# Sparse attention beside the recurrence: two of its steps instead of three per weight unit

## The chip, the cores and the metric

The kernel runs on one core of one Trainium2 chip. The metric is the device time of one execution in microseconds (us). The median of three runs before the change is 1681.42 us (1681.36 to 1682.54).

## The reference, cut to what matters

The program is one block of a first model and two layers of a second one, for 256 tokens of width 1024. The change touches the mixer of the first block alone. That mixer computes two groups of outputs from the same normalised input, joins them and projects them:

```
parts = jnp.split(h @ w_in, IN_SPLITS, axis=-1)
nq, k_c, v_c, k_s, v_s, k_w, v_w, gl, hq, hf, hi, hg = parts
o_nsa = nsa_group(nq, k_c, v_c, k_s, v_s, k_w, v_w, gl, ...)   # sparse attention, 8 heads of 64
o_hg  = hgrn2_group(hq, hf, hi, hg, lower_bound, hg_norm)      # gated recurrence, 4 heads of 128
return jnp.concatenate([o_nsa, o_hg], axis=-1) @ w_out
```

The sparse attention adds three branches, each weighted by a gate: attention to the selected blocks, to the window, and to 15 compressed blocks. With 256 tokens the first two see every earlier token. The recurrence multiplies its state path with `hi` and gates its normalised output with `hg`.

## The kernel before, in words

The 256 tokens are two tiles of 128, called T=0 and T=1. Each tile is a Python generator (`net(T)`) that writes the whole program for that tile; `run` lets T=0 go ahead and T=1 follow some steps behind, so that one weight unit in SBUF serves both. A generator yields the name of the weight unit that it wants next, or None for a step without weights.

A weight unit is one or two pieces of up to 256 KB, which come on SyncE's queue into 6 buffers `wr`. Each piece is split by ScalarE (L319, the rounded high part) and VectorE (L320, the rest) into a pair out of 42 buffers `w`, and a product of activations and weights is three matmuls (`mm3`, L348 to L350, here called weight matmuls, type fp32r). A pair of `w` is free again when T=1 has used it, and ScalarE's split of a later piece waits for that.

Inside the mixer, `merge(main, side, per)` writes `main` up to its next weight unit, then `per` steps of `side`:

```
def merge(main, side, per=1):
    ...
        while True:
            u = yield tag
            tag = main.send(u)
            for _ in range(per):
                next(side, None)
    ...
    for _ in side:
        yield None
```

`main` is `hgrn_out` here: the product `hi` (4 weight units), the recurrence's output (L903, L905), its mean square (ScalarE L907, L912, VectorE L453, GpSimd L455, VectorE L925), the product `hg` (4 units), the gate (ScalarE L922, VectorE L923, L924, L926) and the transpose of the result (`to_xT`: L358, then L353 and L354). `side` is `nsa_attn`: four blocks, one for each of two branches and two halves of the heads, then the compressed branch, then the transpose. A block is three steps: scores (L986) and softmax (VectorE L656, then ScalarE L658, for four heads); transposes of the first probabilities (L358) and a copy (`pT`, ScalarE L673 or VectorE L671), then the first products with the values (L1002); the rest of them and the weighted sum (L962, L963, L970, L974). The compressed branch is L1012, L1019 to L1032, a transpose, L1036 and the sum. In all `nsa_attn` has 14 yields.

After the mixer's two groups comes `out_proj("wo")`, whose weights are 8 row blocks: the first four belong to the attention's half of the input, the last four to the recurrence's half.

PSUM has, for each tile, one bank `mm`, one `tr` and two `a`. Matmuls that are not weight matmuls (type f32: L358, L986, L1002, L903, L905, L1012, L1036) are called f32 matmuls below. The order of the instructions on each engine is fixed when the program is built: a planner orders what the generators write, and functions marked `urgent`, `to_xT` among them, are put ahead.

Of the kernel before, what the change touches and what calls it, by code (L numbers as in the profile page):

```python
# [241 lines left out]
def merge(main, side, per=1):  # L242
    ret = None
    try:
        tag = next(main)
# [5 lines that stand above are left out]
    except StopIteration as e:  # L251
        ret = e.value
    for _ in side:
        yield None
    return ret
# [9 lines left out]
class Net:  # L265
# [416 lines left out]
    def mixer1(self, T, xT, done):  # L682
        nc, sh, c = self.nc, self.sh, self.c
        kn = P * (T + 1)
        tk = slice(P * T, P * T + P)
        oT = self.xt_tiles()


        pz = yield from self.dense("hf", xT, 4, 512)
        zc = self.s2()  # L690
        nc.vector.tensor_scalar(zc, pz, -69.0776, None, op0=OP.max)
        l = self.s2()
        nc.scalar.activation(l, zc, AF.Abs)
        nc.scalar.activation(l, l, AF.Exp, scale=-1.0)
        nc.scalar.activation(l, l, AF.Ln, bias=1.0)
        logf = self.s2()
        nc.vector.scalar_tensor_tensor(logf, zc, 0.0, l, op0=OP.min, op1=OP.subtract)
        nlk = zc
        nc.vector.scalar_tensor_tensor(nlk, zc, 0.0, l, op0=OP.max, op1=OP.add)
        bp = self.pt("tr")  # L700
        for h in range(4):
            nc.tensor.matmul(bp[:, P * h:P * h + P], logf[:, P * h:P * h + P], c["tri"],
                             start=True, stop=True)
        bT = self.s2()
        nc.scalar.activation(bT, bp, AF.Copy)
        up = self.pt("tr")
        for h in range(4):
            self.tr(up[:, P * h:P * h + P], nlk[:, P * h:P * h + P])
        uT = self.s2()
        nc.vector.scalar_tensor_tensor(uT, up, -1.0, bT, op0=OP.mult, op1=OP.subtract)  # L710
        if T == 0:
            kx = self.keep(P, 4).rearrange("p h t -> p (h t)")
            for h in range(4):
                nc.scalar.activation(kx[:, P * h:P * h + P], uT[:, P * h:P * h + P], AF.Exp,
                                     bias=bT[:, P * h + P - 1:P * h + P])
            sh["kx"] = kx


        pz = yield from self.dense("hq", xT, 4, 512, bank="a")
        qs = self.s2()  # L720
        nc.scalar.activation(qs, pz, AF.Tanh, scale=0.5)
        nc.vector.scalar_tensor_tensor(qs, qs, 1.0, pz, op0=OP.add, op1=OP.mult)
        tp = self.pt("tr")
        for h in range(4):
            self.tr(tp[:, P * h:P * h + P], qs[:, P * h:P * h + P])
        qT = self.s2()
        nc.scalar.activation(qT, tp, AF.Copy, scale=0.5)


        pz = yield from self.dense("kk", xT, 4, 512)  # L730
        kk = self.s2()
        nc.scalar.activation(kk, pz, AF.Copy)
        if T == 0:
            sh["kc2"] = self.keep(P, 4)
            sh["nkT"] = self.keep(S, 2)
            sh["nv"] = self.keep(S, 2)
            sh["kcb"] = self.t("kcb", [P, 2, 16], 1)
            nc.gpsimd.memset(sh["kcb"], 0.0)
        cp = self.pt("tr")
        for g in range(4):  # L740
            for lp in range(2):
                nc.tensor.matmul(cp[64 * lp:64 * lp + 64, 64 * g:64 * g + 64],
                                 kk[:, 64 * g:64 * g + 64], c["sel"][:, 64 * lp:64 * lp + 64],
                                 start=True, stop=True)
        kc2 = sh["kc2"]
        nc.scalar.activation(kc2[:, :, 64 * T:64 * T + 64],
                             cp[:, 0:256].rearrange("p (g t) -> p g t", g=4), AF.Copy)
        tp = self.pt("tr")
        for i in range(2):
            self.tr(tp[:, P * i:P * i + P], kk[:, 256 + P * i:256 + P * i + P])  # L750
        nkT = sh["nkT"]
        nc.scalar.activation(nkT[:, :, tk], tp[:, 0:256].rearrange("p (b t) -> p b t", b=2), AF.Copy)

        yield from merge(self.nsa_proj(T, xT, nsa := {}),
                         self.hgrn_levels(T, bT, uT, qT, hg := {}))
        yield from merge(self.hgrn_out(T, xT, hg, oT), self.nsa_attn(T, nsa, oT), 3)
        yield from self.out_proj("wo", [oT], 8, W_WO, done)

    def compress(self):
# [806 lines left out]
```

## Time and profile before

| | |
|---|---|
| median of three runs | 1681.42 us |
| the profiled execution: its time, its span | 1679.82 us, 1678.0 us |
| TensorE busy | 1649.1 us, 98% |
| VectorE busy, ScalarE busy | 1111.4 us (66%), 937.1 us (56%) |
| DMA, mean share of 16 engines on the main queue | 55.8% |
| the chain that ended last | 87% TensorE, 6% VectorE, 3% DMA, 2% ScalarE |

A busy time sums the durations of an engine's instructions. Matmuls overlap, and their ends are modelled, so the distance from one matmul's start to the next one's start says more than a duration. The changed part of the program runs from about 283 to 381 us of the span.

### The profile page before, as it was taken

The numbers are of one execution on the slowest core, as the hardware profiler recorded it, in microseconds if no ns is written. First come the engines' busy times: TensorE is split into PE (matmuls) and PEld (weight loads), VectorE is DVE, ScalarE is ACT, GpSimd is POOL, SyncE is SP. The second block draws the span as 40 slices with busy tenths as digits, with TensorE's granted clock in tenths as the row PEclk, the third lists the DMA queues.
The fourth block names the chain that finished last, engine by engine and source line by source line (L and its number), as shares of the span: only waits on it lengthen the run. The fifth ranks groups of instructions, "written<-read, shape, count | busy, mean of one in ns | idle before, by whom it ended". The sixth has DMA issues, their size and how long they took to land.

```text
span 1678.0 us, 24853 instructions
## 1 busy us (share of the span) xinstructions
PE 1649.1 (98%) x8020; PEld 1343.1 (80%) x8020; DVE 1111.4 (66%) x2309; ACT 937.1 (56%) x1899; POOL 23.8 (1%) x43
## 2 busy tenths in 40 slices
PE   9999999999999999999999999999999999999997
PEld 7888777778888788887888888778888888788886
DVE  7666666676666766677557666885666865766666
ACT  7555655555555555555555555555555775555553
POOL 0000000000000000000000000000000000000000
PEclk9999999999999999999999999999999999999999
DMA  8856544336655566655436565565665633566652
GB/s 280 273 179 176 176 166 126 101 120 195 188 188 178 174 189 189 187 164 164 145 107 213 188 188 188 179 217 168 195 189 163 210 99 100 184 206 189 188 176 76
DMA packets 160547, 293.00 MB, mean 175 GB/s; under 512 B 18208, under 2 KB 27168, under 8 KB 160416
## 3 DMA queue, kind: packets, MB, share of 16 engines
q1 hardware_dynamic: 160128, 291.34, 55.8%
q8 instruction: 63, 1.03, 0.2%
q14 instruction: 68, 0.56, 0.1%
q10 hardware_dynamic: 288, 0.07, 0.0%
HBM read 290.29 MB, written 1.05 MB: 174 GB/s over the span
## 4 chain that ended last, share of the span: by engine, by line
PE 87%; DVE 6%; DMA 3%; ACT 2%; issue 2%; POOL 1%; DVEq 0%; POOLq 0%; SPq 0%; ACTq 0%
PE mm L348 16%; PE mm L350 15%; PE mm L349 15%; PE a L348 10%; PE a L349 9%; PE a L350 9%; PE tr L358 4%; DMA wr<-wp 2%; DVE w L320 1%; DVE x L555 1%; PE a L779 1%; ACT w L319 1%; DVE x L560 1%; DVE x L572 1%; PE a L1294 1%
## 5 line engine op out<-in xcount | busy, mean ns | idle before, releaser
L320 DVE TENSOR_TENSOR w<-wr,w 128x512 fp32r<-128x512 f32 (+3 forms) x1058 | 703.6, 679 | 351.9 <-ACT w L319 165.2
L319 ACT ACTIVATE w<-wr 128x512 fp32r<-128x512 f32 (+3 forms) x1058 | 649.3, 623 | 396.6 <-PE mm L349 233.3
L348 PE MATMUL mm<-w,xh 128*128 128x512 f32 (+3 forms) x1200 | 477.4, 398 | 0.6 <-DVE s L597 0.5
L350 PE MATMUL mm<-w,xl 128*128 128x512 f32 (+3 forms) x1200 | 464.8, 387 | 0.0
L349 PE MATMUL mm<-w,xh 128*128 128x512 f32 (+3 forms) x1200 | 463.8, 387 | 0.0
L348 PEld LDWEIGHTS mm<-w,xh 128*128 128x128 f32 x1200 | 225.7, 188 | 44.6 <-issue 4.4
L350 PEld LDWEIGHTS mm<-w,xl 128*128 128x128 f32 x1200 | 225.5, 188 | 43.3
L349 PEld LDWEIGHTS mm<-w,xh 128*128 128x128 f32 x1200 | 226.2, 189 | 38.7 <-issue 0.6
L348 PE MATMUL a<-w,s 128*128 128x512 f32 x531 | 208.1, 392 | 0.5 <-ACT s L353 0.5
L349 PE MATMUL a<-w,s 128*128 128x512 f32 x531 | 207.4, 391 | 0.0
L350 PE MATMUL a<-w,s 128*128 128x512 f32 x531 | 207.2, 391 | 0.2 <-DVE s L354 0.2
L348 PEld LDWEIGHTS a<-w,s 128*128 128x128 f32 x531 | 99.6, 188 | 25.0 <-issue 3.6
L348 PE MATMUL a<-w,xh 128*128 128x512 f32 (+2 forms) x304 | 118.8, 392 | 0.8 <-ACT xh L353 0.7
L349 PE MATMUL a<-w,xh 128*128 128x512 f32 (+2 forms) x304 | 118.0, 389 | 0.8 <-DVE w L320 0.7
L350 PE MATMUL a<-w,xl 128*128 128x512 f32 (+2 forms) x304 | 116.7, 387 | 0.0
L350 PEld LDWEIGHTS a<-w,s 128*128 128x128 f32 x531 | 99.6, 188 | 21.1 <-DVE s L354 0.6
L349 PEld LDWEIGHTS a<-w,s 128*128 128x128 f32 x531 | 99.7, 188 | 19.9
L353 ACT ACTIVATE s<-tr 128x256 fp32r<-128x256 f32 (+2 forms) x137 | 50.6, 371 | 70.8 <-PE tr L358 70.7
L354 DVE TENSOR_TENSOR s<-tr,s 128x256 fp32r<-128x256 f32 (+2 forms) x137 | 56.5, 413 | 47.9 <-ACT s L353 47.7
L358 PE MATMUL tr<-const,s 128*128 128x128 f32 (+1 forms) x436 | 77.5, 274 | 3.9 <-DVE s L595 1.8
L358 PEld LDWEIGHTS tr<-const,s 128*128 128x128 f32 (+1 forms) x436 | 55.9, 140 | 29.7 <-DVE s L472 2.7
L348 PEld LDWEIGHTS a<-w,xh 128*128 128x128 f32 x304 | 57.1, 188 | 14.8 <-ACT xh L353 3.3
(280 smaller groups left out, 1355.0 us busy)
## 6 DMA issues: line engine op xcount, KB each, us to landing
wr<-wp SPq DMA_DIRECT2D x994, 256.0 KB, 2.7
gb<-vec SPq DMA_DIRECT2D x21, 512.0 KB, 4.3
wr<-wp SPq DMA_DIRECT2D x32, 192.0 KB, 2.4
w<-wp SPq DMA_DIRECT2D x16, 256.0 KB, 5.3
wr<-wp SPq DMA_DIRECT2D x16, 160.0 KB, 2.4
wr<-wp SPq DMA_DIRECT2D x8, 168.0 KB, 2.3
wr<-wp SPq DMA_DIRECT2D x8, 140.0 KB, 2.1
out<-x SPq DMA_DIRECT2D x4, 256.0 KB, 2.0
```

The costliest lines, as they stand in the source:

```text
L319: nc.scalar.activation(hi[:, 0:w], r[:, 0:w], AF.Copy)
L320: nc.vector.tensor_tensor(lo[:, 0:w], r[:, 0:w], hi[:, 0:w].bitcast(FT), op=OP.subtract)
L348: mm(out, xh, wh, start=start, stop=False)
L349: mm(out, xh, wl, start=False, stop=False)
L350: mm(out, xl, wh, start=False, stop=stop)
L353: self.nc.scalar.activation(hi, src, AF.Copy)
L354: self.nc.vector.tensor_tensor(lo, src, hi.bitcast(FT), op=OP.subtract)
L358: self.nc.tensor.transpose(out, src, self.c["ident"][0:n, 0:n])
L555: nc.vector.scalar_tensor_tensor(y[:, cs], y[:, cs], nm, g[:, cs], op0=OP.add, op1=OP.mult)
L560: nc.vector.scalar_tensor_tensor(y[:, cs], y[:, cs], r, b[:, cs], op0=OP.mult, op1=OP.add)
L572: self.nc.vector.scalar_tensor_tensor(x[:, cs], acc, c, x[:, cs], op0=OP.mult, op1=OP.add, accum_out=s)
L779: nc.tensor.matmul(hp[0:2 * nb, 256 * kv:256 * kv + 256], kbs[kv][:, cc].rearrange("p g b -> p (g b)"), u[i][0], start=cc == 0, stop=cc == 15)
```

## The change

```
         yield from merge(self.nsa_proj(T, xT, nsa := {}),
                          self.hgrn_levels(T, bT, uT, qT, hg := {}))
-        yield from merge(self.hgrn_out(T, xT, hg, oT), self.nsa_attn(T, nsa, oT), 3)
+        yield from merge(self.hgrn_out(T, xT, hg, oT), self.nsa_attn(T, nsa, oT), 2)
         yield from self.out_proj("wo", [oT], 8, W_WO, done)
```

`hgrn_out` asks for 8 units, and `merge` writes attention steps after each of units 1 to 7. With three the attention is written out after five units; with two its 14 yields fill all seven places, and its last piece (the transpose of its result) is written after `hgrn_out` has ended, behind the transpose of the recurrence's result. The number of steps that `run` sees is the same, and so is the order of the weight units.

What moves on the engines. First TensorE, where T=1 does its third attention block and the recurrence's product. Before, `tr_974` and `tr_976` are the transposes of the block's probabilities (`se_...`), `a_973` its products with the values, `a_1008` the output projection of T=0 and `a_981` the recurrence's output of T=1:

```order
L348 MATMUL a_1008_3665<-w_3731,xh_2036 128x512
L349 MATMUL a_1008_3665<-w_3732,xh_2036 128x512
L350 MATMUL a_1008_3665<-w_3731,xl_2037 128x512
L358 MATMUL tr_974_3536<-const,se_3519 128x128 x2
L358 MATMUL tr_974_3536<-const,se_3523 128x128 x2
L358 MATMUL tr_976_3543<-const,se_3527 128x128 x2
L358 MATMUL tr_976_3543<-const,se_3531 128x128 x2
L1002 MATMUL a_973_3535<-keep_2425,pT_3541 128x64 x4
L1002 MATMUL a_973_3535<-keep_2425,pT_3548 128x64 x4
L903 MATMUL a_981_3572<-s_980_3570,s_700_2634 128x128
```

Now the same block's transposes are `tr_980` and `tr_982`; `mm_967` is the product `hg` of T=1, and `tr_985` the transpose of the recurrence's result of T=0:

```order
L358 MATMUL tr_980_3558<-const,se_3545 128x128 x2
L349 MATMUL mm_967_3533<-w_3287,xh_2233 128x512
L350 MATMUL mm_967_3533<-w_3286,xl_2234 128x512
L348 MATMUL mm_967_3533<-w_3290,xh_2233 128x512
L349 MATMUL mm_967_3533<-w_3291,xh_2233 128x512
L350 MATMUL mm_967_3533<-w_3290,xl_2234 128x512
L358 MATMUL tr_982_3565<-const,se_3549 128x128 x2
L358 MATMUL tr_982_3565<-const,se_3553 128x128 x2
L358 MATMUL tr_985_3588<-const,s_854_3182 128x128 x4
L1002 MATMUL a_979_3557<-keep_2425,pT_3563 128x64 x4
L1002 MATMUL a_979_3557<-keep_2425,pT_3570 128x64 x4
L358 MATMUL tr_986_3595<-const,s_799_3014 128x128 x4
```

Five weight matmuls now stand between the second and the third transposes, where none stood, and the transposes of T=0's two results (`tr_985`, `tr_986`) have come into this place.

Second TensorE, at the end of T=1's attention. Before, `tr_1020` is the transpose of the compressed branch, `a_1022` its product, `tr_1006` the transpose of the recurrence's result of T=0, and `a_1007` is T=0's output projection again:

```order
L350 MATMUL mm_986_3592<-w_3342,xl_2234 128x512
L358 MATMUL tr_1020_3701<-const,se_3689 128x128
L1036 MATMUL a_1022_3705<-s_774_2918,pT_3703 128x512
L358 MATMUL tr_1006_3657<-const,s_870_3223 128x128 x4
L348 MATMUL a_1007_3664<-w_3751,xh_2036 128x512
```

Now the compressed branch's transpose is `tr_1032`, its product `a_1034`, and T=0's output projection is `a_987` and `a_988`:

```order
L348 MATMUL a_987_3602<-w_3665,xh_2036 128x512
L349 MATMUL a_987_3602<-w_3666,xh_2036 128x512
L358 MATMUL tr_1032_3749<-const,se_3737 128x128
L350 MATMUL a_987_3602<-w_3665,xl_2037 128x512
L348 MATMUL a_988_3603<-w_3669,xh_2036 128x512
L1036 MATMUL a_1034_3753<-s_774_2918,pT_3751 128x512
L349 MATMUL a_988_3603<-w_3670,xh_2036 128x512
L350 MATMUL a_988_3603<-w_3669,xl_2037 128x512
```

Weight matmuls of T=0 now stand between the three f32 matmuls that stood in a row.

Third ScalarE, at the softmax of T=1's second block. Before:

```order
L353 ACTIVATE xh_2036<-tr_906_3327 128x512
L658 ACTIVATE se_3463,col_3456<-se_3463,col_3464 128x256
L658 ACTIVATE se_3467,col_3456<-se_3467,col_3468 128x256
L658 ACTIVATE se_3471,col_3456<-se_3471,col_3472 128x256
L658 ACTIVATE se_3475,col_3456<-se_3475,col_3476 128x256
L673 ACTIVATE pT_3485<-tr_957_3480 128x512
```

Now three splits and a copy of the product `hi` (L899) stand ahead of it:

```order
L319 ACTIVATE w_3768<-wr_3764 128x512
L319 ACTIVATE w_3772<-wr_3766 128x512
L319 ACTIVATE w_3814<-wr_3810 128x512
L899 ACTIVATE s_961_3511<-mm_899_3304 128x512
L658 ACTIVATE se_3456,col_3449<-se_3456,col_3457 128x256
L658 ACTIVATE se_3460,col_3449<-se_3460,col_3461 128x256
L658 ACTIVATE se_3464,col_3449<-se_3464,col_3465 128x256
L658 ACTIVATE se_3468,col_3449<-se_3468,col_3469 128x256
L673 ACTIVATE pT_3484<-tr_956_3479 128x512
```

On all engines together the numbers and shapes of the instructions are the same before and now, and their orders differ only from the first attention blocks up to the start of the next feed-forward part (`f2`).

## Rows read from the trace of the kernel before

**Rows 1.** The page: busy time of TensorE and its weight loads, VectorE, ScalarE, GpSimd (us, share of the span, instructions), and the granted TensorE clock in 40 slices of the span, in tenths of full speed.

```profile
PE 1649.1 (98%) x8020; PEld 1343.1 (80%) x8020; DVE 1111.4 (66%) x2309; ACT 937.1 (56%) x1899; POOL 23.8 (1%) x43
PEclk9999999999999999999999999999999999999999
```

**Rows 2.** Busy time by stretch, for 280 to 370 us: length of the stretch, TensorE, weight loads, VectorE, ScalarE, GpSimd, granted clock, DMA share, GB/s.

```profile
280.00:370.00 90.00, 85.28 (x488) 65.53 (x487) 58.11 (x172) 50.31 (x146) 2.32 (x4) 1.00 0.34 102
```

**Rows 3.** The instructions of TensorE in order of time (start, duration, line, tensors, shapes, count): the scores of T=0's first attention block, and the first matmul of the second chunk of `f2`. Between these two the order of TensorE changes; ahead of the one and from the other on it is the same.

```profile
283.28 0.72 PE L986 MATMUL a<-keep,s 64*128 64x128 f32 x8
...
381.45 0.39 PE L348 MATMUL mm<-w,xh 128*128 128x512 f32 x1
```

**Rows 4.** TensorE in order of time, three places: T=1's scores and the weight matmul behind them; products with the values and the two weight matmuls behind them; two weight matmuls in a row.

```profile
324.95 1.13 PE L986 MATMUL a<-keep,s 64*128 64x256 f32 x8
326.01 0.49 PE L348 MATMUL a<-w,xh 128*128 128x512 f32 x1
...
329.69 1.00 PE L1002 MATMUL a<-keep,pT 128*128 128x64 f32 x8
330.50 0.48 PE L349 MATMUL a<-w,xh 128*128 128x512 f32 x1
330.82 0.40 PE L350 MATMUL a<-w,xl 128*128 128x512 f32 x1
...
366.42 0.39 PE L350 MATMUL a<-w,xl 128*128 128x512 f32 x1
366.65 0.39 PE L348 MATMUL a<-w,xh 128*128 128x512 f32 x1
```

**Rows 5.** The place where T=0's fourth and T=1's first block begin, TensorE, VectorE and ScalarE in order of time; in brackets the engine's idle time before the instruction and what ended it.

```profile
306.95 0.69 DVE L925 TENSOR_TENSOR s<-s,col 128x512 f32<-128x512 f32 x1 [0.93 <-POOL col L455]
307.23 0.70 PE L986 MATMUL a<-keep,s 64*128 64x256 f32 x2
307.56 0.28 DVE L656 CUSTOM_DVE_ANT_0 se<-a,const 128x128 f32<-128x128 f32 x1
307.95 0.40 ACT L658 ACTIVATE se<-se,col 128x128 f32<-128x128 f32 x1 [1.34 <-DVE col L656]
308.49 0.33 PE L358 MATMUL tr<-const,se 128*128 128x128 f32 x1 [0.57 <-ACT se L658]
308.75 0.70 PE L986 MATMUL a<-keep,s 64*128 64x256 f32 x2
309.38 0.33 PE L358 MATMUL tr<-const,se 128*128 128x128 f32 x1
```

**Rows 6.** TensorE in T=1's first block.

```profile
319.67 0.48 PE L350 MATMUL mm<-w,xl 128*128 128x512 f32 x1
320.66 0.43 PE L1002 MATMUL a<-keep,pT 128*128 128x64 f32 x2 [0.51 <-ACT pT L673]
```

**Rows 7.** TensorE in T=1's third block.

```profile
334.38 0.40 PE L350 MATMUL a<-w,xl 128*128 128x512 f32 x1
335.02 0.93 PE L358 MATMUL tr<-const,se 128*128 128x128 f32 x4 [0.25 <-ACT se L658]
336.97 0.66 PE L358 MATMUL tr<-const,se 128*128 128x128 f32 x4 [1.03 <-ACT pT L673]
337.46 2.05 PE L1002 MATMUL a<-keep,pT 128*128 128x64 f32 x16
339.35 0.44 PE L903 MATMUL a<-s,s 128*128 128x128 f32 x2
```

**Rows 8.** TensorE at the end of T=1's attention.

```profile
352.86 0.40 PE L350 MATMUL mm<-w,xl 128*128 128x512 f32 x1
354.45 0.33 PE L358 MATMUL tr<-const,se 128*128 128x128 f32 x1 [1.20 <-ACT se L1027]
355.15 1.13 PE L1036 MATMUL a<-s,pT 128*128 128x512 f32 x2 [0.37 <-ACT pT L673]
356.11 0.60 PE L358 MATMUL tr<-const,s 128*128 128x128 f32 x4
357.40 0.50 PE L348 MATMUL a<-w,xh 128*128 128x512 f32 x1 [0.69 <-ACT xh L353]
```

**Rows 9.** ScalarE and VectorE behind the recurrence's product of T=1 (its last matmul's successor on TensorE starts at 341.29), with a copy `pT` ahead of it.

```profile
336.34 0.57 ACT L673 ACTIVATE pT<-tr 128x512 f32<-128x512 f32 x1
341.39 0.60 ACT L907 ACTIVATE s<-a 128x512 f32<-128x512 f32 x1 [3.99 <-PE a L905]
343.06 0.17 DVE L453 TENSOR_SCALAR col<-col 128x4 f32<-128x4 f32 x1 [2.62 <-ACT s L912]
344.35 0.69 DVE L925 TENSOR_TENSOR s<-s,col 128x512 f32<-128x512 f32 x1 [0.79 <-POOL col L455]
344.96 0.68 DVE L320 TENSOR_TENSOR w<-wr,w 128x512 fp32r<-128x512 f32 x1
345.56 0.42 DVE L656 CUSTOM_DVE_ANT_0 se<-a,const 128x256 f32<-128x256 f32 x1
346.02 0.51 ACT L658 ACTIVATE se<-se,col 128x256 f32<-128x256 f32 x1 [0.33 <-DVE col L656]
```

**Rows 10.** ScalarE at the softmax of T=0's second block: a split, and the first exponential behind it.

```profile
291.54 0.63 ACT L319 ACTIVATE w<-wr 128x512 fp32r<-128x512 f32 x1 [3.50 <-PE mm L349]
292.08 0.39 ACT L658 ACTIVATE se<-se,col 128x128 f32<-128x128 f32 x1
```

More of the change, by code (lines that the diff above doesn't have):

```diff
@@ L755, in mixer1 @@
                          self.hgrn_levels(T, bT, uT, qT, hg := {}))
-        yield from merge(self.hgrn_out(T, xT, hg, oT), self.nsa_attn(T, nsa, oT), 3)
+        yield from merge(self.hgrn_out(T, xT, hg, oT), self.nsa_attn(T, nsa, oT), 2)
         yield from self.out_proj("wo", [oT], 8, W_WO, done)
```

## The prediction

> **What bounds the kernel now.** The page comes first: TensorE is busy for 98% of the span, VectorE for 66%, ScalarE for 56%, and the granted clock is full in every slice [rows 1]. So the time is TensorE's, and a change of order can win only where TensorE stands still. The view by stretch then says how much that is where the change works: of the 90 us from 280 to 370, TensorE is busy for 85.28, at a granted clock of 1.00, which is the 2.4 GHz level [rows 2]. The number of instructions of each shape is the same before and after, so the sum is one of stalls, not of work. Between the first scores and the second chunk of `f2` lie 381.45 - 283.28 = 98.17 us [rows 3]; I ask how much of that is waiting, and how much will be.
>
> For that I read the third view, TensorE in order of time, from start to start. Prices without a wait: 0.23 for a weight matmul, 0.32 for one behind f32 matmuls, so that a change of kind costs some 0.1; 0.81 for four products with the values; 1.06 for T=1's scores, 0.27 for a quarter of them [rows 4]; 0.49 for four transposes, from the start of the second four to what follows them [rows 7]. What a step takes above these prices is a stall. There are four places:
>
> - T=0's fourth and T=1's first block: 308.49 - 307.23 = 1.26 against 0.27, and 309.38 - 308.75 = 0.63 against 0.27. The transposes wait for ScalarE's exponentials, those for VectorE, and VectorE has waited 0.93 for GpSimd's power ahead of L925 [rows 5]. 1.3 us.
> - T=1's first block: 0.99 between a weight matmul and the products, against 0.23 + 0.1; the copy `pT` is late [rows 6]. 0.65 us.
> - T=1's third block: 0.64 against 0.33, then 1.95 against 0.49 (the second transposes wait in the only bank `tr` until ScalarE has copied the first), then 1.89 for eight products against 1.62 [rows 7]. 2.0 us.
> - The end of T=1's attention: 1.59 against 0.33, 0.70 against 0.12, 1.29 against 0.49. The compressed branch runs alone, and the weight matmul behind it needs a transpose of T=0 whose input VectorE finished late [rows 8]. 2.6 us.
>
> Together 6.55 us, and this is the most that any order can win here. The column of idle times gives less for the same places: 0.57, 0.51, 0.25 + 1.03, and 1.20 + 0.37 + 0.69 make 4.62 [rows 5 to 8], because four transposes that took 1.95 are shown as busy for 0.93 and the first 0.3 of a wait is hidden under the modelled end of the matmul ahead. The Trainium skill (Perfetto Trace Analysis, section Tensor Engine Instruction) says that the end of a TensorE instruction is computed and not observed; the trace agrees, with 1.95 from start to start against 0.25 and 1.03 of idle time. By that column as a budget the change would come out at no gain, which is a rival below.
>
> **The change, stall by stall.** Work, weights and DMAs stay, and so does the order of SyncE's queue. In TensorE's new order I counted the changes between weight matmuls and f32 matmuls: 91 instead of 89, at 0.1 each 0.2 us more. The four places go: at the first, GpSimd's power now falls into T=0's third block; at T=1's third block there are weight matmuls of its own `hg` between the transposes; at the end, T=0's output projection lies between the compressed branch's matmuls, and both of T=0's transposes are long done. What comes in their place I worked out by setting the new order of TensorE, ScalarE and VectorE side by side with the durations above. Times count from the end of the matmuls named.
>
> - **GpSimd's power in T=0's third block.** From the end of the recurrence's product ScalarE copies and squares until L453 starts at 343.06 - 341.29 = 1.77; L925 starts 1.29 later, the next VectorE instruction 0.61 after that [rows 9], so the second head's L656 starts at 3.67. From L656 to its transpose were 308.49 - 307.56 = 0.93 us [rows 5]: 4.60. TensorE has fifteen weight matmuls until then, eight of them narrow (280 of 512 columns, counted at that share of 0.23), four scores and one transpose, and is there at 4.1. Then ScalarE has two more copies and a split ahead of `pT`: 0.2 more. 0.7 us.
> - **T=0's fourth and T=1's first block.** They still stand together. Two splits wait for T=1's first `hi` matmuls to free their buffers, and T=0's softmax is behind them on VectorE; I get 0.3 to 0.7, and take 0.5.
> - **T=1's second block.** On ScalarE a split, which must wait for a weight matmul behind the scores, and L899 stand ahead of the exponentials. From the scores' end: split 0.55 to 1.1, L899 to 1.65, first exponential to 2.15 (0.51 long [rows 9]). TensorE has seven weight matmuls, 0.32 + 6 x 0.23 = 1.7, then waits 0.4; and 0.2 for the second. 0.6 us.
> - **T=1's third block**, now with GpSimd's power in it. TensorE waits 0.25 for the squares to leave a bank `a`; the first exponential is behind L922 and a split on ScalarE, 0.2; the second head's L656 comes at 1.77 + 1.29 + 0.61 + 0.60 (L925 and L923 ahead of it) = 4.27, its exponential 346.02 - 345.56 = 0.46 later [rows 9] and ends at 5.24, where five weight matmuls have brought TensorE to 4.95: 0.3. Two more exponentials and the copy `pT` (0.57 [rows 9]) end at 6.9, TensorE is there at 6.7: 0.25 with the transit. 1.0 us where 2.0 were.
> - **Entry to T=1's fourth block**: the scores wait for L970 of the third, behind a split and L354 on VectorE: 0.4 us. In the block a split between the first and second L656 costs 0.45. At the start of T=1's output projection the copy L353 of the attention's transpose, 0.60 long, is covered by one weight matmul and the change of kind: 0.4.
>
> The sum: 0.7 + 0.5 + 0.6 + 1.0 + 0.4 + 0.45 + 0.4 = 4.05, with the changes of kind 4.25, against 6.55. That is 2.3 us less. Nothing later should take it back: from the second chunk of `f2` on the order is the old one and TensorE is the bound, so the gain stays as an earlier end. There the splits run less far ahead than before (T=1 uses the 42 buffers later), but in the new order some twenty weight matmuls, over 4.5 us, still lie between the matmul that frees a pair and the one that needs what is put into it. The profiled execution would take 1679.82 - 2.3 = 1677.5; the median of the runs is 1.60 above the profiled one, so I forecast 1681.42 - 2.3 = **1679.1 us**. What a measurement of this kernel can tell from no change is 0.2%, 3.36 us: the forecast lies within it.
>
> Bounds: each new stall is bounded below by nothing and above by the wait for the compressed branch, 1.59 - 0.33 = 1.26 [rows 8]. Seven at nothing give 6.55 - 0.2 = 6.35 less, 1675.1; seven at 1.26 give 8.8 + 0.2 - 6.55 = 2.5 more, 1683.9. My values lie nearer the lower end, since each was set against filler that the order shows.
>
> **The rivals.**
> - *The waits only move.* By the idle column 4.62 us leave and some 4.25 come: 1681.0 to 1681.4. For it speaks that the same chains (scores, exponentials, copy, products) are all still there; against it, that at two of the four places nothing like the 1.95 and 1.59 is left in the order. Chance 0.18.
> - *Deeper cover.* The waits that hang on splits (0.5, 0.6, 0.45, and 0.4 at the projection) vanish because the splits have run ahead; the chain over GpSimd and the entry stay, 0.7 + 1.0 + 0.4 + 0.2 = 2.3. Then 4.25 less, 1677.2, faster by more than can be told. For it: DMA is at 0.34 of its time here [rows 2], so pieces lie ready. Chance 0.20.
> - *Splits ahead of the softmax* (slower). ScalarE takes its instructions in order. At T=0's second block a split waited 3.50 us for TensorE to free its buffer, and the exponential started only behind it [rows 10]. Now such splits stand ahead of the softmax at two places, T=0's fourth and T=1's second block. If each held it back by 3.50 with no filler left, 7.0 us come on top: 1686.1. It decides the sign for the measurement from 5.6 us on, 2.8 at each. Against it: the matmuls that free those buffers stand just ahead of the scores or one place behind them. Chance 0.12. The Trainium skill (PSUM — Partial Sum Buffer, section Engine vs sequencer instructions) calls ScalarE's and VectorE's queues strictly first in, first out; the exponential at 292.08 behind the split at 291.54 agrees.
>
> **How the numbers follow.** The forecast has a chance of 0.50; it and the first rival, 0.68 together, lie within 0.2%. The deeper cover gives faster with 0.20, the splits slower with 0.12; some of the forecast's own spread goes below -3.36 us, so I say 0.22, 0.66 and 0.12. The range reaches from the lower bound to near the upper, 1675.4 to 1683.6, and leaves out the slower rival and the ends of the bounds.
>
> **What would show it.** Right: the first matmul of the second chunk of `f2` comes 2 to 2.7 us earlier, near 379.1; no step from start to start above 1.3 us at the end of T=1's attention; 1.0 us or less between the transposes of T=1's third block; GpSimd's power inside T=0's third block with a wait of about 0.5. Wrong: that matmul at 381 or later, long idle times of ScalarE ahead of L319 with exponentials behind them, or a gain up to there that is gone again at the end of `f2`.

## The result, and the profile after

The changed kernel takes 1671.85 us (median of six runs, 1670.96 to 1673.44) against 1681.36 us before in the same comparison; the ratio is 0.9949, 95% interval 0.9936 to 0.9962. The forecast was 1679.1 us, the range 1675.4 to 1683.6: the direction was right, the size far too small, and the time lies outside the range. With the experiments below came eleven more executions of the changed kernel and 86 of the one before: the median of the changed kernel's 17 is 1672.27 us and that of the 86 is 1679.97, so the gain is 7.7 us there where the first comparison has 9.5.

The page of the changed kernel, busy times as in [rows 1]:

```profile
PE 1645.7 (99%) x8020; PEld 1342.8 (80%) x8020; DVE 1111.3 (67%) x2309; ACT 937.6 (56%) x1899; POOL 24.1 (1%) x43
```

The stretch from 280 to 370 us, as in [rows 2]; columns as there.

```profile
280.00:370.00 90.00, 88.75 (x518) 70.08 (x518) 62.26 (x181) 54.44 (x152) 3.31 (x5) 1.00 0.38 110
```

TensorE is busy for 88.75 of these 90 us where it was 85.28, and does 518 matmuls in them where it did 488. The two marks of [rows 3], in the changed kernel's TensorE in order of time:

```profile
283.02 0.49 PE L986 MATMUL a<-keep,s 64*128 64x128 f32 x4
...
375.05 0.39 PE L348 MATMUL mm<-w,xh 128*128 128x512 f32 x1
```

From mark to mark, called the **touched part** below, it is 92.03 us where it was 98.17: 6.14 less, with the clock at 1.00 throughout in both. The steps from start to start, summed over the touched part by what stands at the start of each step, say where they went (before, after): the 78 transposes L358 with the waits behind them 10.84, 7.29; the 240 weight matmuls 60.83, 59.46; the 64 records of scores L986 10.20, 8.93; all else 16.30, 16.36. So the transposes gave 3.55, the weight matmuls (by the waits that ended behind one, as at 352.86 in [rows 8]) 1.37, and the scores 1.27. Of the scores, T=0's fourth block with T=1's first went from 3.61 us to 2.12 and T=0's second from 1.06 to 0.65, while T=0's third rose from 0.65 to 1.28 (from the start of the scores to what follows them, so a wait right behind them is in it).

T=0's fourth and T=1's first block, the place of [rows 5]:

```profile
305.40 1.89 PE L986 MATMUL a<-keep,s 64*128 64x256 f32 x16
307.51 0.33 PE L358 MATMUL tr<-const,se 128*128 128x128 f32 x1 [0.23 <-ACT se L658]
```

All scores of both blocks stand in one run here, with no transpose between them. T=1's second and third blocks, the third being the place of [rows 7]:

```profile
319.09 1.14 PE L986 MATMUL a<-keep,s 64*128 64x256 f32 x8
...
328.24 1.13 PE L986 MATMUL a<-keep,s 64*128 64x256 f32 x4
329.29 0.50 PE L349 MATMUL mm<-w,xh 128*128 128x512 f32 x1
...
330.44 1.13 PE L986 MATMUL a<-keep,s 64*128 64x256 f32 x4
331.49 0.50 PE L350 MATMUL mm<-w,xl 128*128 128x512 f32 x1
...
332.29 0.38 PE L358 MATMUL tr<-const,se 128*128 128x128 f32 x2
332.43 0.48 PE L350 MATMUL mm<-w,xl 128*128 128x512 f32 x1
...
333.69 0.44 PE L358 MATMUL tr<-const,se 128*128 128x128 f32 x2
333.88 0.48 PE L349 MATMUL mm<-w,xh 128*128 128x512 f32 x1
...
335.16 0.66 PE L358 MATMUL tr<-const,se 128*128 128x128 f32 x4
335.65 0.60 PE L358 MATMUL tr<-const,s 128*128 128x128 f32 x4
336.08 2.02 PE L1002 MATMUL a<-keep,pT 128*128 128x64 f32 x16
337.94 0.61 PE L358 MATMUL tr<-const,s 128*128 128x128 f32 x4
338.67 1.13 PE L986 MATMUL a<-keep,s 64*128 64x256 f32 x8
```

The second block's four scores (x8: two records for each) run from 319.09 to 320.15 by the start of what follows. The third block's come in two runs of half as many records, and each takes as long: 329.29 - 328.24 = 1.05, 331.49 - 330.44 = 1.05. Before, the first four transposes of the third block started 1.95 us ahead of the second four [rows 7], with nothing between them. Now they come in two pairs, with weight matmuls 0.14 and 0.19 behind them. The second four (335.16) and the four of T=0's result that follow them (335.65) take 0.49 and 0.43, so no wait is left between them. The end of T=1's attention, the place of [rows 8], and the start of its output projection:

```profile
348.61 0.27 PE L358 MATMUL tr<-const,se 128*128 128x128 f32 x1
348.64 0.47 PE L350 MATMUL a<-w,xl 128*128 128x512 f32 x1
...
349.25 1.12 PE L1036 MATMUL a<-s,pT 128*128 128x512 f32 x2
...
356.73 0.47 PE L350 MATMUL a<-w,xl 128*128 128x512 f32 x1
357.66 0.50 PE L348 MATMUL a<-w,xh 128*128 128x512 f32 x1 [0.46 <-ACT xh L353]
```

The compressed branch waits for nothing now: T=0's output projection lies between its matmuls. The step of 0.93 at 356.73, against 0.33, is the largest wait left.

### The profile page after: what moved, and what is told of

It is laid out like the page before. It is cut to its first block, busy times and chain, and to the rows that moved or that the text cites. A ratio compares the mean times of both kernels' runs of the same rounds, so it can differ in the third digit from the quotient of the medians.

```text
span 1669.7 us, 24851 instructions
## 1 busy us (share of the span) xinstructions
PE 1645.7 (99%) x8020; PEld 1342.8 (80%) x8020; DVE 1111.3 (67%) x2309; ACT 937.6 (56%) x1899; POOL 24.1 (1%) x43
## 3 DMA queue, kind: packets, MB, share of 16 engines
q8 instruction: 63, 1.03, 0.2%
HBM read 290.29 MB, written 1.05 MB: 174 GB/s over the span
## 4 chain that ended last, share of the span: by engine, by line
PE 91%; DVE 5%; issue 1%; ACT 1%; DMA 1%; POOL 1%; DVEq 0%; SPq 0%; POOLq 0%; ACTq 0%
PE mm L348 16%; PE mm L350 16%; PE mm L349 16%; PE a L348 10%; PE a L349 10%; PE a L350 10%; PE tr L358 4%; PE a L779 1%; DVE x L555 1%; DVE w L320 1%; PE a L1294 1%; PE a L870 1%; DVE x L560 1%; PE a L1273 1%; DVE x L572 1%
## 5 line engine op out<-in xcount | busy, mean ns | idle before, releaser
L358 PE MATMUL tr<-const,s 128*128 128x128 f32 (+1 forms) x436 | 77.7, 274 | 2.7 <-DVE s L472 1.5
L358 PEld LDWEIGHTS tr<-const,s 128*128 128x128 f32 (+1 forms) x436 | 56.0, 140 | 28.0 <-DVE s L472 2.7
```

The costliest lines, as they stand in the source:

```text
L358: self.nc.tensor.transpose(out, src, self.c["ident"][0:n, 0:n])
```

## The experiments

What all of them gave in one table (touched part and scores from each kernel's trace, from start to start; "1.2 GHz" says whether the granted clock fell to 0.50 inside the touched part; the 86 executions of the kernel before are those made with the experiments; the ratio is to the kernel before, of the first comparison for the changed kernel and of the second for the last row):

| kernel | touched part | scores | 1.2 GHz | median us (executions) | ratio, 95% |
|---|---|---|---|---|---|
| before | 98.17 | 10.20 | no | 1679.97 (86) | |
| before, again | 101.01 | 10.20 | yes | in the row above | |
| changed | 92.03, 92.08, 92.09 | 8.93 | no | 1672.27 (17) | 0.9949, 0.9936 to 0.9962 |
| two steps for T=0 only | 104.27 | 10.49 | yes | 1681.96 (11) | 1.0014, 1.0005 to 1.0023 |
| two steps for T=1 only | 95.51 | 10.19 | no | 1676.38 (11) | 0.9982, 0.9973 to 0.9990 |
| one step | 95.41 | 9.03 | no | 1675.54 (10) | 0.9979, 0.9969 to 0.9990 |
| four steps | 107.24 | 11.67 | yes | 1685.81 (5) | 1.0035, 1.0021 to 1.0048 |
| same half adjacent | 93.20 | 9.39 | no | 1674.22 (6) | 0.9968, 0.9956 to 0.9980 |
| halves together | 97.69 | 7.26 | yes | 1678.48 (11) | 0.9985, 0.9975 to 0.9996 |
| before, wait filled | 99.67 | 10.35 | yes | 1679.65 (12) | 0.9995, 0.9983 to 1.0007 |
| recurrence first | 90.89, 90.87 | 8.93 | no | 1672.26 (12) | 0.9950, 0.9934 to 0.9966 |

### The changed kernel again, twice

No edit.

> The changed kernel once more, beside the others of this call on one chip. Its part that the change touches, from the first scores to the first weight matmul of the second chunk of f2, was 92.03 us in the changed kernel's trace and 98.17 us before (6.1 less); after that point the two programs' TensorE orders are alike, yet the later part was 1.9 us shorter too (1294.65 against 1296.55 us). Theory A: the change is worth the 6.1 us alone, and the 1.9 us are how executions differ from each other; then this run has the touched part within 0.3 us of 92.0 and a later part anywhere from 1294 to 1297, and the ratio over five rounds is 0.9955 to 0.9965. Rival B: the change also shortens what follows (the weights are further ahead); then the later part is again 1294.4 to 1294.9 and the ratio is 0.9945 to 0.9953.

> The changed kernel a third time, beside the two others on one chip: 92.0 to 92.1 us in the touched part by both traces so far, the granted clock full in all of it, and a median of 1671.5 to 1672.5 us.

Measured: 92.08 and 92.09 us in the touched part, 1672.27 and 1672.70 us. The touched part of this kernel repeats to 0.06 us. From its end to the end of the span it was 1294.7 us in the first trace, 1295.7 and 1295.5 in these; before, 1296.6. Over all the kernels here this later part, whose order is the same in all, is 1294.1 to 1298.2 us, so the 1.9 us of the first pair lie within what executions scatter; the two further traces are 0.9 and 1.0 us below the one of before. The first ratio, 0.9952, fell into the window that I had given to theory B, though the later part did not; it left a gain of 7.6 us in the times against 6.1 in the traces, which asked for a second trace of before.

### The kernel before again

No edit.

> The kernel before once more, for its trace: the changed kernel's second trace had the touched part at 92.08 us (92.03 in the first), and its later part 1.1 us longer than in the first. Theory A (the touched part repeats, the rest is scatter of executions): 98.0 to 98.3 us again in the touched part, and the later part (1287.0 us in the first trace, to the last matmul) anywhere from 1284.5 to 1288. Rival B (the later part is systematically longer before the change): 1287 or more again, so that a part of the gain lies behind the touched part.

Measured: 101.01 us in the touched part, outside theory A; the later part 1296.6, the same as in the first trace, as rival B said. Two traces of before at 1296.6 against three of the changed kernel at 1294.7 to 1295.7 leave open whether some 1 us of the gain lies there. The end of T=1's attention in this second trace (TensorE in order of time):

```profile
352.46 0.40 PE L350 MATMUL mm<-w,xl 128*128 128x512 f32 x1
354.06 0.33 PE L358 MATMUL tr<-const,se 128*128 128x128 f32 x1 [1.20 <-ACT se L1027]
354.76 1.82 PE L1036 MATMUL a<-s,pT 128*128 128x512 f32 x2 [0.37 <-ACT pT L673]
356.37 1.06 PE L358 MATMUL tr<-const,s 128*128 128x128 f32 x4
358.11 0.79 PE L348 MATMUL a<-w,xh 128*128 128x512 f32 x1 [0.69 <-ACT xh L353]
```

And its busy times by stretch, granted clock in the third column from the end:

```profile
355.00:356.00 1.00, 1.00 (x2) 0.28 (x2) 1.00 (x5) 0.74 (x2) 0.00 (x0) 0.53 0.00 0
360.00:361.00 1.00, 1.00 (x4) 0.81 (x3) 1.00 (x2) 0.00 (x0) 0.00 (x0) 0.50 0.00 0
778.00:780.00 2.00, 2.00 (x8) 1.57 (x7) 1.37 (x5) 1.43 (x7) 0.00 (x0) 0.58 0.00 0
```

The waits are those of [rows 8] to the hundredth (1.20, 0.37, 0.69). But behind them the clock falls to 0.50, the 1.2 GHz level, for some 7 us, and weight matmuls take 0.43 instead of 0.23: 2.84 us more. In the first trace the same waits stood there with the clock at 1.00. So the waits before the change cost not only their length: in this execution the clock fell behind them. It fell once more at 778.3 us, behind the touched part, for 3.4 us; four other traces below have such a fall near there, none of them one of the changed kernel or of the order with the recurrence first. The times agree: of 86 executions of before 40 had a mean granted clock of 0.998 or more over the span, median 1678.69 us, and 29 had 0.996 or less, down to 0.993 at 1686 us; of 17 of the changed kernel 14 had 0.998 or more, median 1671.99, and none less than 0.997. Among the executions with 0.998 or more, called undisturbed below, the difference is 6.7 us; over all 7.7. About 1 us of the gain therefore goes with the clock. Where in the span it fell in the executions without a trace is not shown.

### Which tile gains: T=0 only, T=1 only

```diff
-        yield from merge(self.hgrn_out(T, xT, hg, oT), self.nsa_attn(T, nsa, oT), 2)
+        yield from merge(self.hgrn_out(T, xT, hg, oT), self.nsa_attn(T, nsa, oT), 3 - (T == 0))
```

> Two steps for the first 128 tokens (T=0) only, three still for T=1. By the trace of the changed kernel the touched part lost 1.27 us of scores (matmuls of 64 partitions each, which run side by side when the two halves alternate back to back) and about 4.9 us of waits. In this kernel the scores stand as in the changed kernel (the same groups), so that term is here whole. Theory A (each tile's waits are covered by its own spread): the waits near 306 and 320 us go (about 2), those near 336 and 341 to 357 us (4.6 before) stay, so the touched part is 98.2 - 1.3 - 2 = about 95 us (94.3 to 95.7) and the time 3 us under before. Rival B (T=1's waits went because T=0's output projection came later, beside them): nearly all of the gain is here, 92 to 93 us.

Measured: 104.27 us in the touched part and 1681.96 us, against 1679.47 for before in the same comparison, so slightly slower; both theories fail. T=1's third block in this kernel (TensorE in order of time), and the busy times by stretch around it:

```profile
325.44 1.14 PE L986 MATMUL a<-keep,s 64*128 64x256 f32 x8 [0.52 <-DVE s L970]
327.73 1.18 PE L358 MATMUL tr<-const,se 128*128 128x128 f32 x4 [1.15 <-ACT se L658]
329.68 1.11 PE L358 MATMUL tr<-const,se 128*128 128x128 f32 x4 [0.77 <-ACT pT L673]
```

```profile
325.00:330.00 5.00, 2.58 (x14) 1.50 (x15) 2.19 (x11) 2.92 (x10) 0.00 (x0) 0.80 0.23 73
330.00:335.00 5.00, 5.00 (x25) 5.00 (x24) 1.51 (x3) 0.11 (x1) 0.00 (x0) 0.50 0.00 0
```

Scores, transposes and products stand in a row with no weight matmul between them. The reason is T=0's output projection: before, it began at 322.36 and covered T=1's middle blocks (at 326.01 in [rows 4]); with T=0's attention spread to the end of its own units it starts only at 357.27, and behind 323.28 the next of T=1's own weight matmuls comes at 338.96. The clock falls behind the waits and stays at 0.50 until about 338, and it falls again from 352 to about 359, behind waits of 1.20 and 0.37. The trace shows more than the times do: 6.1 us in the touched part against 2.5 us in the medians.

```diff
-        yield from merge(self.hgrn_out(T, xT, hg, oT), self.nsa_attn(T, nsa, oT), 2)
+        yield from merge(self.hgrn_out(T, xT, hg, oT), self.nsa_attn(T, nsa, oT), 3 - (T == 1))
```

> Two steps for T=1 only, three still for T=0. The scores of T=0 stand as before the change (mostly apart), only T=1's gain: some 0.3 us. Theory A (each tile's waits are covered by its own spread): the waits near 306 and 320 us stay, those of T=1 near 336 and 341 to 357 us shrink from 4.6 to about 1.3, so the touched part is 98.2 - 0.3 - 3.3 = about 94.6 us (94.0 to 95.2) and the time 3.5 us under before. Rival B (the order of T=0 decides T=1's waits): under 1 us gained, 97.3 us or more.

Measured: 95.51 us, 1676.38 us: 2.7 of the 6.1 us, just short of theory A's range. The end of T=1's attention:

```profile
357.13 0.39 PE L350 MATMUL a<-w,xl 128*128 128x512 f32 x1
358.90 1.26 PE L358 MATMUL tr<-const,s 128*128 128x128 f32 x8 [1.38 <-DVE s L926]
```

1.77 us remain here from start to start, and 1.27 at the third block (336.58 to 337.85): T=0's projection, begun at 321.40, is used up by 357, before T=1's recurrence is done. So the tiles do not add up: T=0 alone loses, T=1 alone gains 2.7, both gain 6.1. By the orders, T=1's spread puts its own `hg` units where T=0's projection was, and T=0's spread keeps that projection for T=1's end.

### More and fewer steps

The same line with 1, and with 4.

> One step of the attention beside each weight unit, for both tiles. The recurrence's input and gate products have eight units; the attention has some fourteen steps, so at one each about half of it is left when they end, and T=1's half has only T=0's output projection beside it, and in the end nothing. Theory A (what counts is that the attention ends with the units, not after them): the waits at T=1's end return, 4 us or more with the clock possibly at its lower level in them, and the touched part is 95 to 104 us. Rival B (more work of other kinds beside each step is always better): 90 to 92 us.

> Four steps of the attention beside each weight unit. The attention is done after about four of the eight units, and the other units stand alone behind it. T=0's four groups of scores have their halves together here, T=1's first group all apart. Theory A (fewer units beside the attention leave its softmax waits open, as before the change and more so): 98 to 102 us in the touched part. Rival B (the way the groups' halves fall is what decided between three steps and two): scores 9.0 to 9.5 us and the touched part 93 to 96 us.

Measured with one step: 95.41 us, theory A at its lower end. TensorE is busy for 45.00 us of 280 to 325 and then for 16.75 of the 20 us from 325 to 345, at a granted clock of 1.00 in both, where the rest of both tiles' attention stands alone behind the units. With four steps: 107.24 us, worse than theory A; between 335 and 355 the clock is at 0.57 and 0.58 on average, behind waits of 1.15, 1.03, 1.15 and 0.78 at T=1's third and fourth blocks. Scores were 11.67 in it, partly by the clock, so the second theory's number cannot be tested there; its touched part is refuted. Of the counts one to four, two has the shortest touched part; it is the one with which the attention's 14 yields just fill the seven places.

### What the halves of the scores cost

L986 multiplies 64 partitions at a time, and a group of four scores has two for each half of the partitions. The first edit exchanges the loops, so that the two matmuls of a half are neighbours:

```diff
-                for ii in range(2):
-                    for par, sp in enumerate(sps):
+                for par, sp in enumerate(sps):
+                    for ii in range(2):
```

> The changed kernel with the two loops around the scores exchanged: the two matmuls of one half of the partitions (rows 0 to 63, or 64 to 127) stand next to each other, so two of a group's four neighbours no longer alternate. Nothing else moves but by this. Theory A (scores are cheap only where the halves alternate back to back): a T=1 group of 4 was 1.05 us alternating and each lone one about 0.53; with one alternating neighbour left in the middle a T=1 group costs about 1.6 and a T=0 group about 0.95, so eight groups cost some 0.5 x 4 + 0.3 x 4 = 3.2 more than if all were alternating, of which the changed kernel lost two groups' share already: the scores rise from 8.93 to about 11.2 us, and the touched part to 93.5 to 94.3 us (a part of it falls into waits that are there). Rival B (the gain was in the waits alone, scores cost by their columns): scores 8.7 to 9.2 and the touched part 91.8 to 92.4 us.

Measured: scores 9.39 (8.93 before the edit), touched part 93.20. Theory A's size fails, and its wording with it; the 9.39 and 93.20 lie a little above rival B's ranges as well. T=1's second block:

```profile
319.74 1.14 PE L986 MATMUL a<-keep,s 64*128 64x256 f32 x8
320.81 0.50 PE L350 MATMUL mm<-w,xl 128*128 128x512 f32 x1
```

1.07 us, as with alternating halves (1.06): it is enough that both halves stand in one run with nothing else between them. In the records the starts then come in pairs 14 ns apart, against 7 ns when the halves alternate. Only where T=0's scores came between T=1's two halves did the edit cost anything in scores: the run of sixteen records at 305.43 takes 2.55 us instead of 2.11 to the next transpose. The rest of the 1.17 us are waits that moved.

The second edit makes the halves meet, in the two groups of the changed kernel in which they still stood apart because the recurrence's output held one of the two banks `a`:

```diff
+            sh["oread", T] = nc.scalar.activation(junk[:, hs], op[:, hs], AF.Square, ...)
...
                             self.after(m, freed)
                             freed = None
+                            if ("oread", T) in sh:
+                                self.after(m, sh.pop(("oread", T)))
```

> The changed kernel, where the first score matmul of the group that follows the recurrence's output also waits for the last read of that output's bank, so that both halves of each group find their banks free at once. In the changed kernel two groups still ran with the halves apart: T=0's third (2 + 2 matmuls) and T=1's third (328.24 and 330.44 us, 1.05 us each, where a group whose halves are together takes 1.06 in all). Theory A (scores are dear only where the halves stand apart, and TensorE has weight matmuls enough while the group waits): scores fall from 8.93 to about 7.3 us and the touched part from 92.05 to 90.4 to 91.2 us. Rival B (the first half's earlier scores were what kept T=1's chain of softmaxes fed): the 1.6 us come back as waits at the third block's transposes, 91.8 to 92.8 us.

Measured: scores 7.26, as theory A said, and the touched part 97.69, 5.6 more, beyond theory B; 1678.48 us, 6.2 more than the changed kernel. T=0's third block, T=1's third block, and the stretch behind it:

```profile
300.17 0.39 PE L350 MATMUL mm<-w,xl 128*128 128x512 f32 x1
301.14 0.33 PE L358 MATMUL tr<-const,se 128*128 128x128 f32 x1 [0.58 <-ACT se L658]
...
331.10 1.14 PE L986 MATMUL a<-keep,s 64*128 64x256 f32 x8
...
333.43 0.40 PE L349 MATMUL mm<-w,xh 128*128 128x512 f32 x1
335.30 0.44 PE L358 MATMUL tr<-const,se 128*128 128x128 f32 x2 [1.47 <-ACT se L658]
```

```profile
340.00:345.00 5.00, 5.00 (x19) 4.22 (x19) 2.77 (x6) 1.11 (x2) 0.00 (x0) 0.52 0.43 117
```

At T=1's third block the four scores cost 1.07 instead of 2.10, but the first half's softmax no longer begins 2.2 us ahead of the second's (328.24 and 330.44 in the changed kernel). The first transposes now come 1.87 behind the weight matmul ahead of them, against 0.23 without a wait, and the clock falls behind that. The early half was what fed the chain. At T=0's third block, whose halves the edit also joins, the first transpose comes 0.97 behind the weight matmul, against 0.57 in the changed kernel. The 5.6 us are these waits and the lower clock together; what each is worth was not measured apart.

### One wait of before filled with work

One matmul that computes nothing of use, its result overwritten by the next:

```diff
-        pT, = self.pTs([s], P)
         op = self.pt("a")
+        if T == 1:
+            nc.tensor.matmul(op, c["ident"], sh["vbd"].rearrange("p h d -> p (h d)"), start=True, stop=True)
+        pT, = self.pTs([s], P)
```

> The kernel before with one matmul more (128x512, f32, some 0.9 us of TensorE) put into the 1.2 us wait for the compressed branch of T=1; its result is overwritten by the product that follows, so it is work for nothing. Theory A (in the kernel before the clock falls to 1.2 GHz behind the waits from 352 to 358 us in a part of the executions, as in its second trace: 2.8 us; and this is the 1.3 us by which the timed gain exceeds the 6.1 us of the two first traces): the wait shrinks by what the matmul takes, the touched part stays at 98.1 to 98.4 us, the clock is full throughout it, and the median over the executions is under that of the kernel before, 1678.0 to 1679.2 us. Rival B (the waits cost only their own length): the touched part is the same but for 0.1, and the median is that of before, 1679.5 to 1680.3 us, or over it.

Measured: 99.67 us and 1679.65 us, ratio 0.9995; both of theory A's numbers fail; the time lies in rival B's range, the touched part does not. The added matmul came at 353.08, the wait at the place shrank from 1.20 to 0.34 us, and no fall of the clock followed it, as none did in the first trace of before; but in this trace it fell at another place, behind the waits of [rows 5]:

```profile
307.97 0.33 PE L358 MATMUL tr<-const,se 128*128 128x128 f32 x1 [0.58 <-ACT se L658]
...
355.43 0.33 PE L358 MATMUL tr<-const,se 128*128 128x128 f32 x1 [0.34 <-ACT se L1027]
```

```profile
309.00:310.00 1.00, 1.00 (x5) 0.82 (x5) 0.78 (x2) 0.20 (x1) 0.00 (x0) 0.50 0.57 111
```

The highest of 12 executions was 1681.60 us, against 1686.39 among 17 of before on the same chip (lowest granted clock 0.996 against 0.993), which would fit the theory that this place makes the long falls. Neither that nor the median shows it: the interval contains 1.

### The recurrence's half first in the output projection

```diff
-    rows = [((64 * i, 64 * (i + 4)), None) for i in range(4)] + row_blocks(8)[4:]
+    rows = row_blocks(8)[4:] + [((64 * i, 64 * (i + 4)), None) for i in range(4)]
...
-            self.mm3(accs[j], (hi[:, k % 8, :], lo[:, k % 8, :]), w, k == 0, k == n - 1)
+            m = (k + 4 * (tag == "wo")) % 8
+            self.mm3(accs[j], (hi[:, m, :], lo[:, m, :]), w, k == 0, k == n - 1)
```

> The changed kernel with the row blocks of the mixer's output projection in another order: the recurrence's half of the input first, then the attention's. In the changed kernel T=1's projection begins with the attention's half, whose copy L353 TensorE awaits 0.46 us at 357.66, while the recurrence's half was transposed 2.5 us before. Theory A: that wait goes and nothing else moves; the touched part is 91.4 to 91.8 us and the time 0.3 to 0.6 us under the changed kernel's. Rival B: T=0's projection, which now also begins with the other half, takes a wait of its own, 92.0 us or more.

> The changed kernel with the recurrence's half first in the output projection, once more. Its first trace had the touched part at 90.89 us (the changed kernel's three traces: 92.03, 92.08, 92.09), but its median of 1672.64 us was the changed kernel's (1672.70). Theory A (the 1.2 us repeat and are worth their time; the first six executions scattered): 90.8 to 91.0 us again and a median of 1670.8 to 1671.8 us. Rival B (what is won there is lost in the later part, where TensorE waits for other chains): the same touched part, a later part of 1296 us or more, and a median of 1672.2 us or more.

Measured: 90.89 and 90.87 us in the touched part, and the wait at the projection is gone:

```profile
356.34 0.39 PE L350 MATMUL a<-w,xl 128*128 128x512 f32 x1
356.57 0.43 PE L348 MATMUL a<-w,xh 128*128 128x512 f32 x1
```

The 1.2 us repeat, twice what I expected and outside both ranges of the first run, but the median of 12 executions is 1672.26 against 1672.27 for the changed kernel, and the later part (1295.7, 1295.6) is no longer than that kernel's. The touched part began 0.4 us later than in the changed kernel's traces (283.40, 283.36 against 282.64 to 283.02). Neither theory of the second run has both of its numbers. A gain of this size is below what these runs tell, and whether it is one stays open.

## Why the prediction was wrong

**The bound was right, and the four places in the main.** TensorE is the bound, the weight matmuls of T=1's own `hg` and of T=0's output projection took the waits at T=1's third block and at its end, and nothing was given back in `f2`. The mark forecast for 379.1 came at 375.05. From the start of the touched part it was to come 2.3 us earlier and came 6.14 earlier, 3.84 more.

**The step that failed first: the new waits were sized too large.** 4.05 us were forecast, about 1.9 came, which is 2.1 of the 3.84. Against the prices of [rows 4] and [rows 7], in the changed kernel: the power in T=0's third block 0.7, came 0.24 (300.68 to 301.25, against 0.33); T=0's fourth with T=1's first block 0.5, came 0.29; T=1's second block 0.6, came 0.12 to 0.2; T=1's third block 1.0, came nothing (335.16 to 336.08 above); the entry to the fourth block 0.4, came 0.13 to 0.24 (337.94 to 338.67, against 0.49); inside it 0.45, came 0.43 to 0.52; the start of T=1's output projection 0.4, came 0.6 to 0.7. The last two were about right, and 0.29 is the lower end of the 0.3 to 0.7 that I had given.

At the third blocks I took the two halves of a group as released together, while the halves apart both filled TensorE longer and started half of the softmax chain 2 us early. The run with the halves together shows it: there the wait that I forecast at T=1's third block stands, at 1.6 us, and at T=0's third block the first transpose waits 0.64 above its price, where 0.7 was forecast. At T=1's second block the halves stand together, and something else failed. There I let a split of ScalarE wait for a weight matmul behind the scores. In the changed kernel's trace (ScalarE in order of time) the splits were done before the scores ended at 320.15:

```profile
317.81 2.02 ACT L319 ACTIVATE w<-wr 128x512 fp32r<-128x512 f32 x3 [1.82 <-PE mm L349]
320.69 0.60 ACT L899 ACTIVATE s<-mm 128x512 f32<-128x512 f32 x1 [0.86 <-PE mm L350]
321.18 0.50 ACT L658 ACTIVATE se<-se,col 128x256 f32<-128x256 f32 x1
```

The first exponential ends 1.5 us behind the scores, where I had 2.15. Why the entry to T=1's fourth block came cheaper was not looked into.

**"The sum is one of stalls, not of work" failed.** The same instructions are not the same work: the scores' two halves run side by side if nothing separates them, and one after the other if something does. The wrong step is the price of 0.27 for a quarter of T=1's scores, a division of 1.06 by four [rows 4]. One half alone takes 1.05, so a lone quarter costs some 0.5 to 0.6. [Rows 5] had it in sight: both steps of "0.70 ... x2" there are 0.63 at least without any wait. Of the 1.3 us of stalls read at that place 0.7 was work, and it left with the run of sixteen records. So most of the scores' gain stood in the sum under a wrong name. Of the 1.27 us, 0.35 is a shorter wait behind them (0.94 behind the scores at 307.55 before, 0.60 at 306.91 after) and 0.9 is work; only some 0.2 of the 3.84 comes from here.

**The list of waits was not complete.** Three smaller ones of the kernel before were on none of the four places: 0.43 from 326.81 to 327.24 and 0.44 from 346.24 to 346.68, against 0.23, and 0.61 for the four transposes at 371.86, against 0.36. They left too, some 0.6 of the 3.84. The remaining 0.9 is spread over small steps and not assigned.

**The cost of a wait was taken as its length alone, and for the kernel before this failed.** [Rows 2] showed a clock of 1.00 and I reasoned from that one execution (the digit 9 of [rows 1] says only 90% or more). The second trace of the same program has 2.84 us of lower clock behind the same waits. No term of the sum and no rival had this; about 1 us of the 7.7 goes with the clock, and so the 6.55 us that I called the most that any order can win was no cap on the time. The start was off as well: the 1681.42 from which I subtracted was the median of three executions, 1.45 above that of the 86 later ones.

**The rivals.** Waits that only move, and splits ahead of the softmax, are both refuted: the waits of the places above were some 5.8 us before and 1.9 after, and the softmax of T=1's second block runs with a wait of at most 0.2. Deeper cover (1677.2) was the nearest, in that most of the new waits vanished. The reason it named, splits that have run ahead, holds at T=1's second block by the rows above, and is not what was shown at the third blocks; it also lacked the clock. The bound from below, 6.35 us less, lies close to the 6.14 of the touched part by luck: it counted 0.7 of work as waits, left out the three smaller waits, and had no new waits at all where 1.9 came. For the time it did not hold.

**What stays open.** Traces give 6.1 us, the times with an undisturbed clock 6.7; the 0.6 between them lies within the scatter of the later part and was not told apart from it.

## What to carry to other kernels

Before a change of order is priced as waits alone, look for instructions whose cost depends on their neighbours: compare a group in one run with the same group cut in two, from start to start, instead of dividing the group's time by its count. When two streams cover each other's waits, a change to one of them moves what the other was covered by; try them together, since here one alone lost and both gained more than the sum. And take a second trace of the kernel before: here the same waits cost only their length in one execution, and stood ahead of a lower clock in the next.

## What the runs showed of the hardware

- Matmuls on 64 partitions of the two halves overlap: eight records in 1.06 us, four of one half alone in 1.05. They need not alternate: with two of one half ahead of two of the other it is 1.07, and records start 14 ns apart in pairs, instead of 7. The Trainium skill (TensorE: Matmul & The Clock Gate, section The mechanism) says that matmuls on different row groups overlap, which the rows agree with, and that matmuls start strictly in program order. With the second they do not agree. One half's four records start 0, 0.32, 0.54 and 0.75 us into its run (from 328.24). In strict order the other half's four would begin behind these, and the group would take some 0.75 + 1.05 = 1.8 us, not 1.07. The records do not name their half, so this is inferred from the total.
- The same program with the same waits (1.20, 0.37 and 0.69 us of idle time within 6 us) kept 2.4 GHz in one execution and fell to 1.2 GHz for 7 us in another.
